# A hybrid decoder layer on one core: the first pair's running sums use one buffer fewer, and the last gate's SiLU stands five products later

## The chip, the cores and the metric

One NeuronCore of a Trainium2 chip runs the whole layer in one launch. The metric is the device time of one execution in microseconds (us). The engines are named as the profile names them: PE is TensorE, DVE is VectorE, ACT is ScalarE, POOL is GpSimd, and SP issues most of the DMAs. Each engine works through its own instructions in a fixed order; an instruction that waits holds up all that stand behind it on its engine.

## The reference

One sequence of 1024 tokens, width 1024, float32. The layer is a SwiGLU half-step, a mixing step, and a second SwiGLU half-step; each has a norm before and after, and shift, scale and gate from a conditioning vector `c`:

```python
c_act = silu(c); mod = c_act @ w_ada + b_ada          # nine rows of 1024
f = (silu(h @ w_gate) * (h @ w_up)) @ w_down          # 1024 -> 2816 -> 1024
x = x + 0.5 * ga1 * rms_norm(f, g_post_ff1)
attn = sliding_window_attention(q, k, v, sinks)       # 8 heads, window 128
ssm = s5_ssm(u, ...)                                  # 32 groups, 64 complex states each
x = x + ga2 * rms_norm(concat(norm(attn), norm(ssm)) @ w_out, g_post_mix)
f = swiglu(h, w2_gate, w2_up, w2_down)
x = x + 0.5 * ga3 * rms_norm(f, g_post_ff2)
```

## The kernel before

**Precision and products.** Every large float32 product is done as three matmuls of a faster format: an operand is split into a high part (an ACT cast, L69) and a low part (a DVE subtraction, L70), and `mm3` (L74 to L76) multiplies high by high, high by low and low by high. The low part of the weights is needed by the third matmul, L76.

**Gate and up projections.** `GateUp` computes them with Strassen's scheme in Winograd's form: the activations stand as 2x2 blocks (512 tokens by 512 channels), the weights too, and a pair of 128-column output tiles (u = 0, 1) needs seven products of 12 matmuls each instead of eight. The first pair is done plainly (`first`); all others go through `rest`, one product after the other in the order "1", "5", "6", "2", "7", "3", "4". Products 1, 6, 7 and 4 add up in one PSUM bank (chain 0), and between them the partial sum is copied out: product 1's by ACT L470 into buffer `c11`, product 5's by L472 into `c22`, product 6's by L474 into `c12`. So the matmuls of product 6 may not begin before L470 has read the bank, and those of product 7 not before L474 has. "Product 6" in the change's words is the sixth in order, product "3".

**Running sums.** The down projection uses the same scheme, so the four result blocks of a pair are stored together with four sums of them. `sums` makes them on DVE (L429, in the order s3, s1, s2, s4) and SP stores them. For the first pair `first_done(1)` calls it, ahead of `rest`, with high priority in the scheduler.

**Buffers.** The blocks and sums live in eight buffers h0 to h7 that `o_rot` hands out in turn. In the first feed-forward the first pair's blocks take h0 (a11), h1 (a12), h2 (a21), h3 (a22), and the four sums h4 to h7; the next request, `c11` of `rest`, gets h0 again. The second feed-forward does the same, one place on: a11 is in h7 there and so is `c11`. A later pair takes exactly eight buffers, so the relation repeats.

**Order.** Inside `rest` each product's steps are pinned in the order written: the conversion of the weights three products ahead (`conv`), the product, a hook. Elsewhere a scheduler that simulates the program chooses each engine's order from dependences and priorities; a change in one place can so move instructions in another. The h buffers also serve the attention's split probabilities in mixing (`at_turn`, L785 and L70), where the state-space steps (`ss_state`, L893 to L916, DVE and POOL) run beside attention; `at_values` multiplies the split probabilities by the values (L74 to L76).

**The last gate.** `hook3` loads `c` once more through POOL (L117), takes its SiLU on ACT (L118, 128x1024), loads the last eight rows of `w_ada` through POOL (L162) and reduces them on DVE (L166) from the tenth product on.

Of the kernel before, what the change touches and what calls it, by code (L numbers as in the profile page):

```python
# [30 lines left out]
def tile_layer(ctx: ExitStack, tc: tile.TileContext, a: dict, out: bass.AP, stage: str = "all"):  # L31
# [12 lines left out]
    def slot(tag, shape, dt=F32):  # L44
        uid[0] += 1
        return sb.tile([P] + list(shape), dt, tag=tag, name=f"{tag}_{uid[0]}")
# [18 lines left out]
    def names(c, *idx):  # L65
        return tuple(f"{c}{i}" for i in idx)
# [31 lines left out]
    o_rot = Rot(*names("h", *range(8)))  # L98
# [15 lines left out]
    def load_c(eng):  # L114

        crow = slot("c0", [D])
        tc.keep_in_program_order(eng.dma_start(crow, a["c"].partition_broadcast(P)))  # L117
        act.activation(crow, crow, AF.Silu)  # L118
        return crow
# [40 lines left out]
    def ada_load(j, tag):  # L160
        w = slot(tag, [D])
        pool.dma_start(w, a["w_ada"][j])  # L162
        return w

    def ada_block(j, w, crow=crow):
        return dve.tensor_tensor_reduce(w, w, crow, 1.0, b_ada[:, j : j + 1], MUL, ADD, modc[:, j : j + 1])  # L166
# [9 lines left out]
    def gate_row(n, v, half):  # L176
        g = ggc[:, n, :]
        if half:
            dve.scalar_tensor_tensor(g, mod(v), 0.5, gains[:, 2 * n + 1, :], op0=MUL, op1=MUL)
        else:  # L180
            dve.tensor_tensor(g, mod(v), gains[:, 2 * n + 1, :], op=MUL)

    def gate_store(n):
        pt = bank(tr_rot(), [P])
        pe.transpose(pt[0:8, :], ggc[:, n, :], ident)
        act.copy(rows[:, n, :], pt[0:8, :])
        pool.dma_start(row_d[n].rearrange("(k p) -> k p", p=P), rows[:, n, :])
# [171 lines left out]
    class GateUp:  # L359
# [49 lines left out]
        def first_done(self, r):  # L409
            for f in range(2):  # L410
                s = slot(o_rot(), [512])
                act.activation(s, self.pb[r, 0, f], AF.Silu)
                dve.tensor_tensor(s, s, self.pb[r, 1, f], op=MUL)
                self.result(0, r, f, s)
            if r == 1:
                with tc.high_priority():
                    self.sums(0, [slot(o_rot(), [512]) for _ in range(4)])


        def result(self, pair, r, f, s):  # L420
# [1102 lines left out]

    def hook3(i):

        if not last_c:
            last_c.append(load_c(pool))
        while last_ada and len(last_raw) < 3:
            j = last_ada.pop(0)
            last_raw.append((j, ada_load(j, rest_rot())))  # L1530
        if last_raw and i > 8 and i % 2:
            ada_block(*last_raw.pop(0), last_c[0])
        if i == 40:
            gate_row(2, 8, True)
        if i == 44:
            gate_store(2)

    g2.rest(lambda i: pinned(hook3, i), pinned)
    down(2, a["w2_d"], None, lambda i: None, lambda: None)

# [72 lines left out]
```

## Time and profile before

| what | us |
|---|---|
| median of 3 runs (1717.0 to 1725.35) | 1717.06 |
| the profiled execution, its own time | 1718.82 |
| its span, first to last instruction | 1717.0 |
| PE busy in the span | 1652.9 (96%) |
| DVE, ACT, POOL busy | 1264.6, 804.3, 124.8 |

The profiled execution's own time is 1.82 us more than its span, and 1.76 us more than the median. The stages in the span: the first feed-forward to about 690 us (its first pair until about 83 us), mixing to about 1060, the second feed-forward from there (its first pair until about 1112). A row of the timeline gives start, duration, engine, line, operation, names and shapes; in brackets the idle time before it on its engine and what ended it. `x4` behind a row stands for four instructions in one row, whose duration then runs from the first start to the last end. Granted clock 1.00 is 2.4 GHz, 0.50 is 1.2 GHz.

### The profile page before, as it was taken

The page shows a single profiled execution, that of the slowest core. Times are in us where ns is not written, and L with a number is a line of the kernel's source. Part 1 is how long each engine was busy: PE and PEld are TensorE (multiplying, and loading weights), DVE is VectorE, ACT ScalarE, POOL GpSimd, SP SyncE. Part 2 cuts the span into 40 slices and gives each one's busy share as a digit, 9 for nine tenths or more (in the row PEclk, how much of TensorE's full clock was granted, in tenths as well). Part 3 has the DMA queues.
Part 4 walks back from the last instruction along what each step waited for, and adds up shares of the span by engine and source line. Part 5 has one row for each costly group of instructions (what it writes and reads, how often), then busy time and mean ns, then how long its engine had stood idle before and what let it go on. Part 6 is the DMA issues. An engine that isn't in the chain of part 4 may idle for free.

```text
span 1717.0 us, 22221 instructions
## 1 busy us (share of the span) xinstructions
PE 1652.9 (96%) x7669; PEld 1355.8 (79%) x7669; DVE 1264.6 (74%) x2470; ACT 804.3 (47%) x1654; POOL 124.8 (7%) x147
## 2 busy tenths in 40 slices
PE   5999999999999999899979998999999999999998
PEld 4878888787788878688757876878888888888886
DVE  7989997788779878735589378768666566678586
ACT  5633333553344557736555257633333333344562
POOL 0011100001100000000015044000000000000001
PEclk9999999999999999999989998999999999999999
DMA  9176752234395734410333126243232223494324
GB/s 377 42 257 239 244 187 93 104 129 149 128 368 183 232 115 147 150 37 13 96 90 87 49 76 197 84 172 117 104 117 92 93 92 120 154 375 125 110 97 161
DMA packets 112065, 249.08 MB, mean 145 GB/s; under 512 B 12088, under 2 KB 27744, under 8 KB 111952
## 3 DMA queue, kind: packets, MB, share of 16 engines
q1 hardware_dynamic: 102224, 214.12, 36.2%
q0 software_dynamic: 9152, 32.49, 5.6%
q8 instruction: 60, 0.98, 0.2%
q10 hardware_dynamic: 576, 1.05, 0.2%
q14 instruction: 53, 0.43, 0.1%
HBM read 187.87 MB, written 59.75 MB: 144 GB/s over the span
## 4 chain that ended last, share of the span: by engine, by line
PE 51%; DVE 4%; DMA 2%; ACT 1%; issue 1%; POOL 1%; SPq 0%; DVEq 0%; ACTq 0%; POOLq 0%
PE b L76 15%; PE b L75 15%; PE b L74 15%; PE b L751 1%; PE b L839 1%; PE b L841 1%; PE b L840 1%; PE b L785 1%; DMA r<-in_w_gu 1%; PE b L930 0%; PE b L205 0%; DMA w<-in_w_out 0%; ACT a L69 0%; POOL a L913 0%; PE b L926 0%
## 5 line engine op out<-in xcount | busy, mean ns | idle before, releaser
L74 PE MATMUL b<-a,w 128*128 128x512 f32 x1260 | 489.3, 393 | 15.1 <-ACT h L470 9.0
L75 PE MATMUL b<-a,w 128*128 128x512 f32 x1260 | 494.6, 392 | 5.6 <-DVE a L70 5.6
L76 PE MATMUL b<-a,w 128*128 128x512 f32 x1260 | 494.5, 392 | 1.4 <-DVE w L70 1.3
L74 PEld LDWEIGHTS b<-a,w 128*128 128x128 f32 x1260 | 238.0, 189 | 68.6 <-ACT h L470 11.5
L75 PEld LDWEIGHTS b<-a,w 128*128 128x128 f32 x1260 | 238.5, 189 | 56.3 <-DVE a L70 7.0
L76 PEld LDWEIGHTS b<-a,w 128*128 128x128 f32 x1260 | 238.6, 189 | 53.6 <-DVE w L70 3.8
L70 DVE TENSOR_TENSOR w<-r,w 128x512 fp32r<-128x512 f32 (+1 forms) x206 | 142.9, 694 | 137.9 <-ACT w L69 137.6
L75 PE MATMUL b<-w,r 128*128 128x512 f32 x528 | 205.5, 389 | 1.1 <-DVE w L70 1.1
L76 PE MATMUL b<-w,r 128*128 128x512 f32 x528 | 205.4, 389 | 0.0
L74 PE MATMUL b<-w,r 128*128 128x512 f32 x528 | 180.7, 389 | 0.0
L69 ACT CAST w<-r 128x512 fp32r<-128x512 f32 (+1 forms) x210 | 130.2, 623 | 94.3 <-DVE r L334 82.4
L69 ACT CAST r<-a 128x512 fp32r<-128x512 f32 x110 | 68.5, 623 | 149.5 <-PE b L76 107.8
L70 DVE TENSOR_TENSOR r<-a,r 128x512 fp32r<-128x512 f32 x110 | 75.7, 688 | 61.7 <-ACT r L69 61.6
L75 PEld LDWEIGHTS b<-w,r 128*128 128x128 f32 x528 | 99.1, 188 | 22.2 <-DVE w L70 1.6
L74 PEld LDWEIGHTS b<-w,r 128*128 128x128 f32 x528 | 99.1, 188 | 20.6
L76 PEld LDWEIGHTS b<-w,r 128*128 128x128 f32 x528 | 99.1, 188 | 20.5
L69 ACT CAST w<-t 128x512 fp32r<-128x512 f32 (+1 forms) x114 | 69.9, 613 | 83.7 <-DVE t L337 30.4
L70 DVE TENSOR_TENSOR w<-t,w 128x512 fp32r<-128x512 f32 (+1 forms) x114 | 79.7, 699 | 31.5 <-ACT w L69 31.3
L466 DVE TENSOR_TENSOR h<-h,b 128x512 f32<-128x512 f32 x120 | 82.2, 685 | 21.3 <-PE b L76 19.2
L454 ACT ACTIVATE h<-h 128x512 f32<-128x512 f32 x60 | 38.0, 633 | 117.8 <-DVE h L466 117.8
L70 DVE TENSOR_TENSOR w<-a,w 128x512 fp32r<-128x512 f32 x110 | 75.3, 685 | 0.2 <-ACT w L69 0.2
L74 PE MATMUL b<-a,a 128*128 128x512 f32 x182 | 72.2, 399 | 0.1
(376 smaller groups left out, 2554.4 us busy)
## 6 DMA issues: line engine op xcount, KB each, us to landing
r<-in_w_gu SPq DMA_DIRECT2D x88, 512.0 KB, 3.9
g_d<-h SPq DMA_DIRECT2D x154, 256.0 KB, 2.1
a<-g_d SPq DMA_DIRECT2D x110, 256.0 KB, 3.4
q<-in_w_ada POOLq DMA_DIRECT2D x48, 512.0 KB, 4.7
a<-in_w_d SPq DMA_DIRECT2D x88, 256.0 KB, 5.4
a<-in_w_ada SPq DMA_DIRECT2D x16, 512.0 KB, 10.2
a<-in_x SPq DMA_DIRECT2D x12, 512.0 KB, 6.8
x_d<-a SPq DMA_DIRECT2D x12, 512.0 KB, 3.7
```

The costliest lines, as they stand in the source:

```text
L69: act.copy(hi, src)
L70: eng.tensor_tensor(lo, src, hi.bitcast(F32), op=SUB)
L74: pe.matmul(psum, wh, xh, start=first, stop=False, skip_group_check=goes_on)
L75: pe.matmul(psum, wh, xl, start=False, stop=False, skip_group_check=goes_on)
L76: pe.matmul(psum, wl, xh, start=False, stop=last, skip_group_check=goes_on)
L454: act.activation(dst, src, AF.Silu)
L466: dve.tensor_tensor(dst, dst, pb, op=ADD)
L751: pe.matmul(pb[kv][:, m % 2, ks], qT[m][rows, t * P : (t + 1) * P], kT[rows, (t + 1 - nk) * P : (t + 1) * P], start=True, stop=True,)
L785: pe.transpose(pt[:, m, :], pr[4 * kv + m][:, b * P : (b + 1) * P], ident)
L839: pe.matmul(pb, hh, wh, start=k == 0, stop=False)
L840: pe.matmul(pb, hh, wl, start=False, stop=False)
L841: pe.matmul(pb, hl, wh, start=False, stop=k == NK - 1)
```

## The change

In the first pair s1 = a21 + a22 is written over a21 itself; only three buffers are taken for the sums, so `c11` of `rest` gets the eighth. `hook3` returns at once for the first five products, so the load of `c`, its SiLU and the first loads of `w_ada` stand behind the sixth.

```diff
             if r == 1:
                 with tc.high_priority():
-                    self.sums(0, [slot(o_rot(), [512]) for _ in range(4)])
+                    self.sums(0, [self.st[1, 0]] + [slot(o_rot(), [512]) for _ in range(3)])
...
     def hook3(i):
 
+        if i < 5:
+            return
         if not last_c:
             last_c.append(load_c(pool))
```

DVE, first feed-forward, the end of the first pair (a name begins with the tile's tag: `h0` is buffer h0; w2 is the weights of product 6, w3 of product 2, w0 of product 7). Before:

```order
L70 TENSOR_TENSOR w2_143_705<-t0_142_703,w2_143_705 128x512
L70 TENSOR_TENSOR a6_160_821<-q2_4_101,a6_160_821 128x512
L70 TENSOR_TENSOR a7_161_824<-q3_5_102,a7_161_824 128x512
L429 TENSOR_TENSOR h6_156_805<-h0_138_688,h2_152_796 128x512
L429 TENSOR_TENSOR h4_154_803<-h2_152_796,h3_153_799 128x512
L429 TENSOR_TENSOR h5_155_804<-h4_154_803,h0_138_688 128x512
L429 TENSOR_TENSOR h7_157_806<-h1_139_692,h5_155_804 128x512
L70 TENSOR_TENSOR w3_168_854<-r1_135_682,w3_168_854 128x512
L339 TENSOR_TENSOR r0_134_680<-r1_135_682,r0_134_680 128x512
L70 TENSOR_TENSOR w0_171_873<-r0_134_680,w0_171_873 128x512
```

The same place of the changed kernel:

```order
L70 TENSOR_TENSOR w2_143_705<-t0_142_703,w2_143_705 128x512
L70 TENSOR_TENSOR a6_159_820<-q2_4_101,a6_159_820 128x512
L70 TENSOR_TENSOR a7_160_823<-q3_5_102,a7_160_823 128x512
L429 TENSOR_TENSOR h5_155_804<-h0_138_688,h2_152_796 128x512
L70 TENSOR_TENSOR w3_167_853<-r1_135_682,w3_167_853 128x512
L339 TENSOR_TENSOR r0_134_680<-r1_135_682,r0_134_680 128x512
L429 TENSOR_TENSOR h2_152_796<-h2_152_796,h3_153_799 128x512
L429 TENSOR_TENSOR h4_154_803<-h2_152_796,h0_138_688 128x512
L429 TENSOR_TENSOR h6_156_805<-h1_139_692,h4_154_803 128x512
L70 TENSOR_TENSOR w0_170_872<-r0_134_680,w0_170_872 128x512
```

The weights' split for product 2 and one sum of weights moved between the first and the second running sum; the second sum writes h2, which it reads. The second feed-forward has the same new order.

DVE in mixing, about 884 to 892 us of the span before: the state-space step of group 0 (L913 to L915), the probabilities of attention tile 7 (L774, scaled) and of tile 6 (L70, split for `at_values`). Before:

```order
L914 TENSOR_TENSOR a5_1280_7685<-a5_1280_7685,q2_1260_7614 128x512
L772 RECIPROCAL s1311_7792<-s1311_7792 128x8
L804 TENSOR_REDUCE t1_1319_7877<-t0_1316_7852 128x128
L915 TENSOR_TENSOR a8_1315_7843<-a4_1279_7684,a5_1280_7685 128x4x127
L774 TENSOR_SCALAR a17_1303_7768<-a17_1303_7768,s1311_7792 128x256 x2
L774 TENSOR_SCALAR c0_1304_7769<-c0_1304_7769,s1311_7792 128x256 x2
L774 TENSOR_SCALAR a17_1303_7768<-a17_1303_7768,s1311_7792 128x256 x2
L774 TENSOR_SCALAR c0_1304_7769<-c0_1304_7769,s1311_7792 128x256 x2
L897 TENSOR_TENSOR a4_1279_7684<-b5_1334_7919,q3_1283_7688 128x512
L70 TENSOR_TENSOR h0_1323_7888<-b0_1321_7882,h7_1322_7887 128x512
```

The same place of the changed kernel:

```order
L914 TENSOR_TENSOR a5_1279_7684<-a5_1279_7684,q2_1259_7613 128x512
L70 TENSOR_TENSOR h7_1322_7887<-b0_1320_7881,h6_1321_7886 128x512
L772 RECIPROCAL s1310_7791<-s1310_7791 128x8
L70 TENSOR_TENSOR h1_1325_7896<-b1_1323_7890,h0_1324_7895 128x512
L915 TENSOR_TENSOR a8_1314_7842<-a4_1278_7683,a5_1279_7684 128x4x127
L897 TENSOR_TENSOR a4_1278_7683<-b5_1333_7918,q3_1282_7687 128x512
L70 TENSOR_TENSOR h3_1328_7905<-b2_1326_7899,h2_1327_7904 128x512
L70 TENSOR_TENSOR h5_1331_7914<-b3_1329_7908,h4_1330_7913 128x512
L774 TENSOR_SCALAR a17_1302_7767<-a17_1302_7767,s1310_7791 128x256 x2
L774 TENSOR_SCALAR c0_1303_7768<-c0_1303_7768,s1310_7791 128x256 x2
L774 TENSOR_SCALAR a17_1302_7767<-a17_1302_7767,s1310_7791 128x256 x2
```

All four splits of tile 6 now stand ahead of the eight scalings of tile 7.

POOL in mixing, the state-space step of group 1 (its result goes to a9; a8 held group 0's, which PE reads, and is cleared by L916 for group 2). Before:

```order
L894 MEMSET a6_1281_7686 128x4
L913 TENSOR_TENSOR a6_1281_7686<-a4_1279_7684,q3_1283_7688 128x512
L914 TENSOR_TENSOR a6_1281_7686<-a5_1280_7685,q3_1283_7688 128x512
L915 TENSOR_TENSOR a9_1335_7946<-a6_1281_7686 128x4x127
L916 MEMSET a8_1393_8187 128x4 x2
```

The same place of the changed kernel:

```order
L894 MEMSET a6_1280_7685 128x4
L916 MEMSET a8_1392_8186 128x4 x2
L913 TENSOR_TENSOR a6_1280_7685<-a4_1278_7683,q3_1282_7687 128x512
L914 TENSOR_TENSOR a6_1280_7685<-a5_1279_7684,q3_1282_7687 128x512
L915 TENSOR_TENSOR a9_1334_7945<-a6_1280_7685 128x4x127
```

The clearing of a8 moved ahead of group 1's three operations.

## Rows read from the trace of the kernel before

**Rows 1.** Busy time by stretch: the stretch and its length, busy us (and instructions) of PE, PEld, DVE, ACT, POOL, then the granted clock, the DMA share and GB/s.

```profile
0.00:100.00 100.00, 78.38 (x376) 66.13 (x377) 82.70 (x207) 53.64 (x115) 4.12 (x13) 0.95 0.59 225
...
300.00:400.00 100.00, 98.73 (x447) 79.98 (x447) 83.20 (x158) 49.88 (x105) 7.46 (x14) 1.00 0.38 132
...
800.00:900.00 100.00, 88.73 (x482) 69.32 (x481) 64.48 (x187) 56.35 (x196) 6.93 (x11) 0.93 0.26 79
...
1100.00:1200.00 100.00, 95.33 (x412) 78.08 (x412) 79.36 (x126) 39.78 (x69) 4.25 (x8) 0.98 0.38 133
1300.00:1400.00 100.00, 100.00 (x443) 82.81 (x442) 64.94 (x99) 34.17 (x60) 0.00 (x0) 1.00 0.34 119
```

**Rows 2.** Who waited for whom, PE over the whole span: us in total, times, longest.

```profile
PE b L74 <- ACT h L470: 9.0, 5, 4.3
...
PE b L75 <- DVE h L70: 5.2, 1, 5.2
```

**Rows 3.** Timeline of PE, first feed-forward: the last matmul of product 5, the first of product 6, the first of product 2.

```profile
88.32 0.39 PE L76 MATMUL b<-a,w 128*128 128x512 f32 x1
91.23 0.50 PE L74 MATMUL b<-a,w 128*128 128x512 f32 x1 [2.52 <-ACT h L470]
...
95.67 0.39 PE L74 MATMUL b<-a,w 128*128 128x512 f32 x1
```

**Rows 4.** Timeline of DVE at the same place: the weights' split for product 6 and the four running sums.

```profile
86.69 0.69 DVE L70 TENSOR_TENSOR w<-t,w 128x512 fp32r<-128x512 f32 x1
...
88.50 2.74 DVE L429 TENSOR_TENSOR h<-h,h 128x512 f32<-128x512 f32 x4
```

**Rows 5.** Timeline of ACT at the same place.

```profile
84.31 1.15 ACT L69 CAST a<-q 128x512 fp32r<-128x512 f32 x2
90.59 0.59 ACT L470 COPY h<-b 128x512 f32<-128x512 f32 x1 [5.13 <-issue]
```

**Rows 6.** Timeline of PE, second feed-forward: the last matmul of product 5 and the first of product 6.

```profile
1117.27 0.39 PE L76 MATMUL b<-a,w 128*128 128x512 f32 x1
1121.91 0.50 PE L74 MATMUL b<-a,w 128*128 128x512 f32 x1 [4.25 <-ACT h L470]
```

**Rows 7.** Busy time by stretch, columns as in rows 1: behind the two stalls (the second row is product 6 of the second feed-forward, whole), and two stretches of mixing.

```profile
92.03:95.67 3.64, 3.64 (x10) 2.83 (x9) 1.69 (x3) 0.78 (x2) 0.00 (x0) 0.53 0.99 361
1121.91:1126.35 4.44, 4.44 (x12) 3.50 (x13) 2.00 (x4) 2.52 (x4) 0.00 (x0) 0.62 0.99 324
880.00:897.00 17.00, 7.61 (x37) 5.72 (x38) 17.00 (x29) 10.00 (x30) 5.93 (x5) 0.62 0.29 91
897.00:912.00 15.00, 15.00 (x104) 11.81 (x103) 14.30 (x18) 8.18 (x19) 6.21 (x7) 0.98 0.45 123
```

**Rows 8.** Timeline of DVE, second feed-forward: the weights' split for product 6 and the four running sums.

```profile
1117.97 0.69 DVE L70 TENSOR_TENSOR w<-t,w 128x512 fp32r<-128x512 f32 x1
...
1119.17 2.74 DVE L429 TENSOR_TENSOR h<-h,h 128x512 f32<-128x512 f32 x4
```

**Rows 9.** Timeline of ACT, second feed-forward; the last row is the cast of weights that now stands right behind the SiLU.

```profile
1121.27 0.59 ACT L470 COPY h<-b 128x512 f32<-128x512 f32 x1 [6.34 <-issue]
1121.75 1.06 ACT L118 ACTIVATE c<-c 128x1024 f32<-128x1024 f32 x1
...
1136.49 0.61 ACT L69 CAST w<-r 128x512 fp32r<-128x512 f32 x1
```

**Rows 10.** Timeline of PE in mixing, the rows that had waited.

```profile
883.00 1.12 PE L888 MATMUL b<-a,q 128*64 128x128 f32 x16 [2.11 <-ACT r L802]
885.91 0.59 PE L806 MATMUL b<-ones,t 128*128 128x1 f32 x2 [1.79 <-DVE t L804]
...
892.36 0.80 PE L75 MATMUL b<-h,a 128*128 128x512 f32 x1 [5.23 <-DVE h L70]
```

**Rows 11.** Timeline of DVE in mixing.

```profile
885.78 0.73 DVE L915 TENSOR_TENSOR a<-a,a 128x508 f32<-128x508 f32 x1
886.43 2.70 DVE L774 TENSOR_SCALAR a<-a,s 128x256 f32<-128x256 f32 x2
...
891.03 0.68 DVE L897 TENSOR_TENSOR a<-b,q 128x512 f32<-128x512 f32 x1
891.63 0.68 DVE L70 TENSOR_TENSOR h<-b,h 128x512 fp32r<-128x512 f32 x1
892.23 0.14 DVE L807 COPY ss_a<-b 128x1 f32<-128x1 f32 x1
...
895.28 0.68 DVE L70 TENSOR_TENSOR h<-b,h 128x512 fp32r<-128x512 f32 x1
```

**Rows 12.** Timeline of POOL in mixing.

```profile
902.53 1.28 POOL L913 TENSOR_TENSOR a<-a,q 128x512 f32<-128x512 f32 x1 [12.69 <-issue]
...
907.11 0.14 POOL L916 MEMSET a<- 128x4 f32 x2
...
919.54 0.14 POOL L916 MEMSET a<- 128x4 f32 x2 [10.66 <-PE b L930]
921.15 6.28 POOL L913 TENSOR_TENSOR a<-a,q 128x512 f32<-128x512 f32 x1 [1.48 <-issue]
```

**Rows 13.** Who waited for whom, PE from 300 to 400 us.

```profile
PE b L74 <- ACT h L470: 1.1, 1, 1.1
```

**Rows 14.** Timeline of POOL ahead of the second feed-forward: the load of `c`.

```profile
1071.69 0.62 POOL L117 DMA_DIRECT2D c<-in_c  x1 [4.79 <-DVE a L255]
```

## The prediction, made before the changed kernel ran

> **What bounds the kernel now.** I read the busy times by stretch first. In the projections PE is the bound: from 1300 to 1400 us it is busy all 100 us, with 443 matmuls at granted clock 1.00, so a matmul costs 100/443 = 0.2257 us and a product of 12 costs 2.71 us. The stretches 0 to 100, 800 to 900 and 1100 to 1200 stand out: lower PE busy time and a granted clock of 0.95, 0.93 and 0.98 [rows 1]. The PE waits name what is behind it: L74 waits for ACT L470, 9.0 us in five waits, longest 4.3, and L75 waits once for DVE L70, 5.2 us [rows 2]. So any gain must come from a place where PE stands still, and from the matmuls that run at the lower clock after it.
>
> The timeline shows two of the L470 waits at the changed place. In the first feed-forward product 6 could have started at 88.55 us (the last matmul of product 5 starts at 88.32 and issues for 0.23), and started at 91.23 [rows 3]. In the second, product 5 ends at about 1117.50 and product 6 starts at 1121.91 [rows 6]. ACT had nothing to do in either case: L470 stood "issue"-idle for 5.13 and 6.34 us [rows 5, 9], and ran when the DVE sums let go of its buffer: `c11` is h0 (h7 in the second feed-forward), which is a11, and the third sum reads a11. The sums run 88.50 to 91.24 and 1119.17 to 1121.91 [rows 4, 8], and L470 starts at 90.59 and 1121.27, when the third of four is done. A second loss follows: behind the wait PE ran at 0.53 (1.2 GHz for nearly all of it) from 92.03 to 95.67, and product 6 of the second feed-forward took 4.44 us for 12 matmuls at 0.62 [rows 7].
>
> **The change part by part.**
>
> *First feed-forward, edit 1.* In the changed kernel `c11` gets the one buffer that the sums no longer take, so L470 waits for product 1 alone. ACT is free at 85.46 [rows 5], product 1 ends at about 86 us (its successor product 5 takes 2.71 and ends at 88.55), so the copy is done by 86.6 and product 6 starts at 88.55. Its weights' split is done at 87.38 [rows 4]. Without the wait the clock stays up, so product 2 starts at 88.55 + 2.71 = 91.26 instead of 95.67 [rows 3]: **4.4 us**. The lower bound is the bare wait, 91.23 - 88.55 = 2.7.
>
> What is late next? In the new order the split for product 2 and one sum of weights (L339) come between the sums. From 88.50 with 0.6 us a step: s3, split, L339, then s1, s2, s4 from 90.30; s2, the third sum, ends at about 91.7. Now `c22` has a11's buffer, so L472 waits for that: 91.7 to 92.3; behind it on ACT are the cast for product 7 to 92.8 and L474 (`c12` in a12's buffer, whose last reader s4 ends at 92.2) to 93.3. Product 7 needs L474 and would start at 91.26 + 2.71 = 93.97. So 0.7 us are to spare; the price if it is gone is what exceeds it.
>
> *Second feed-forward, edit 1.* The split for product 6 runs 1117.97 to 1118.66 [rows 8], later than PE now arrives (1117.50), and the third matmul needs it: a wait of 0.2 to 0.75 us takes the place of the 4.25. The sums follow from 1119.17, the third ends at 1122.34 in the new order, and L472, cast and L474 end at 1123.0, 1123.5 and 1124.0. Product 7 would be ready at about 1123.4 and so waits some 0.6. Before, it began at 1126.35 + 2.71 = 1129.06; now at about 1124.0: **5.0 us**, bounds 4.0 and 5.9 (no such waits). These short waits need not lower the clock: from 300 to 400 PE waited 1.1 us for the same L470 [rows 13] and the granted clock is 1.00 [rows 1].
>
> *Edit 2, the SiLU.* It issues no DMA where the program text suggests: the load of `c` stands at 1071.69 on POOL [rows 14], 40 us ahead of `rest`; POOL's order is not altered there. What moves is ACT L118, 1.06 us from right behind L470 to ahead of the cast at 1136.49 [rows 9]. With L470 gone from 1121 the SiLU would have run in ACT's idle 6.34 us, so it gains nothing of its own. Weights are converted three products ahead of their use, at 2.71 us each, so a cast that stands 1.06 us later is still early and the rest of PE's work covers it. **0**, bounds -0.6 and +1.1 (all of it in the chain L470, L472, L474 against all of it in front of product 9).
>
> *Mixing, a side effect of edit 1.* The rotation of h buffers is shifted and the scheduler orders differently. The dearest place on PE there is 880 to 897: busy 7.61 of 17.00 us at clock 0.62 [rows 7], with waits of 2.11 (ACT L802), 1.79 and 5.23 (DVE L70) [rows 10]. From 897 PE is busy all the time [rows 7], so what it does earlier is won. Before, the first split for tile 6 stood at 891.63 behind L915, all eight L774 (886.43 to 891.03) and L897 [rows 11]. Now it is ahead of them: 891.63 - 4.60 - 0.60 - 0.65 = 885.8, that is 5.8 us earlier, and the fourth at 889.0 against 895.28. On the other side the L774 end some 3.1 us later (at 894.2), and their transposes (L785) wait for them; and DVE is busy 17.00 of 17.00 and then 14.30 of 15.00 [rows 7], so it can't serve all earlier. The price isn't in the trace. From above it is 9.4 us, PE's idle time 17.00 - 7.61; from below -4, if the 3.1 us of the late L774 and one 0.7 us split come fully onto PE. I take **4.5**, nearer to the rows on the wait that goes (5.23) than to either end.
>
> The Trainium skill, "SBUF — State Buffer", section "Who interferes with whom", speaks against this part: VectorE shares one port pair with GpSimd, and one of them locks out the other, so vector work that is moved onto GpSimd's stretch stretches both. The trace agrees as far as it goes: POOL's L913 took 1.28 us at 902.53 and 6.28 at 921.15 for the same shape [rows 12]. By that rule the step of group 1 may cost up to 5.0 us more on POOL, and the sum would be 4.5 + 4.4 with nothing left of mixing, that is near rival B.
>
> *Sum.* 4.4 + 5.0 + 0 + 4.5 = 13.9. The profiled execution's span of 1717.0 becomes 1703.1 and its own time, 1.82 more, 1704.9. That execution is 1.76 above the median of the runs shown, so on the median's scale: 1717.06 - 13.9 = **1703**.
>
> **The rivals.** B: both waits go, mixing gives back as much as it wins. For it: DVE is full there; against it: PE is full from 897 on, so that early work isn't lost. 1717.06 - 9.4 = 1707.7.
>
> C: the waits are handed on. `c22` and `c12` now stand in a11's and a12's buffers, so L472 and L474 are tied to the same sums that held L470, one product later. If PE's turn came 1 to 2 us before the sums were done in both places, and the clock fell with it, the two gains would shrink from 9.4 to some 5: 1712. For it: the second feed-forward is already 0.6 us short by my count; against it: 0.7 us to spare in the first, and 300 to 400 us with 1.1 us of wait and a full clock [rows 1, 13].
>
> D, slower: POOL's L916 clears a8 for group 2 and waits for PE's L930 of group 0 (at 919.54 it had stood 10.66 us for L930 [rows 12]). It is now ahead of group 1's L913 to L915. If PE's L930 comes late because it stands behind matmuls that wait for the late L774, POOL's 1.28 + 1.72 + 1.60 us start late, L913 may take 6.28 instead of 1.28, and PE's matmuls of group 1 wait. It makes the kernel slower when mixing loses more than the 9.4 won; with the 10.66 wait, 5.0 for L913 and 2.3 of matmuls at the lower clock, 18: 1717.06 - 9.4 + 18 = 1725.7. Against it: before, L913 ran only at 902.53, after 12.69 us of idle time [rows 12], and by then L930 of group 0, ahead of it in PE's order, is nearly done.
>
> **How the numbers follow.** Forecast 0.58, own range 1698 to 1707 (mixing 0 to 9, second feed-forward 4.0 to 5.9); B 0.22; C 0.13; D 0.07. A measurement of this kernel can tell 0.5% from no change, 8.6 us: faster is below 1708.5, slower above 1725.6. Faster takes the forecast, and B with some two thirds (it lies 0.8 us inside the line): 0.72. Same takes the rest of B, C, and the half of D that loses less than 18 us: 0.24. Slower: 0.04. The range leaves out most of D, the best cases of the forecast and the far end of C: 1697 to 1711.
>
> **What would show it.** Right: in the changed trace L470 runs at about 86 and 1115 and waits for PE only; the PE waits for L470 lose 6.8 us of 9.0; granted clock 1.00 from 84 to 100 and 1117 to 1127; at most two PE waits under 1 us before product 7, on L474, and a short one on L70 in the second feed-forward. Mixing right: the 5.23 us wait for L70 is gone and PE is busy over 11 us of 880 to 897; wrong: L785 waits for L774 there, or POOL's L916 shows a wait for L930 with L913 behind it. L118 stands near 1131 and nothing waits for the cast behind it. Wrong altogether: a PE wait of over 1.5 us for L474 or L472 behind the sums, or new idle time in a stage that the change doesn't name.

## The result and the profile after

The changed kernel takes 1705.70 us (median of 4 runs, 1704.67 to 1708.09); the kernel before, beside it, 1720.26 (4 runs, 1717.0 to 1725.35). The ratio is 0.9914, with a 95% interval of 0.9893 to 0.9935. In a later set, beside three variants, the two medians are 1708.88 and 1718.11, ratio 0.9946 (0.9929 to 0.9964). So the change makes the kernel faster by 0.5 to 0.9%: 9 to 15 us, with 13.9 forecast. The span of the profiled execution fell from 1717.0 to 1702.9 us.

The busy times by stretch, columns as in [rows 1], with the stretches of [rows 1, 7]:

```profile
84.00:100.00 16.00, 16.00 (x72) 13.28 (x71) 13.88 (x23) 6.49 (x12) 3.90 (x7) 1.00 0.87 305
880.00:897.00 17.00, 14.90 (x77) 11.23 (x76) 17.00 (x29) 9.21 (x19) 5.46 (x5) 0.80 0.25 79
1100.00:1200.00 100.00, 98.09 (x431) 80.19 (x430) 76.51 (x121) 39.63 (x70) 4.23 (x8) 1.00 0.41 145
874.74:891.74 17.00, 11.63 (x53) 8.17 (x50) 17.00 (x31) 10.96 (x32) 6.00 (x5) 0.80 0.37 123
891.74:906.74 15.00, 13.69 (x112) 10.53 (x113) 15.00 (x18) 11.65 (x24) 5.75 (x7) 1.00 0.48 130
```

From 84 to 100 PE is busy all 16 us and the granted clock is 1.00: the stall of [rows 3] and the slow stretch of [rows 7] behind it are gone. At 870 us this trace is 5.26 us ahead of that of before (the lead is explained below), so the stretch 880 to 897 holds later work than that of [rows 7]. The last two rows are shifted by that lead and hold the same work as 880 to 897 and 897 to 912 before. There PE is idle for 5.4 and 1.3 us, where it stood still for 9.4 and 0.0 us before; the granted clock is 0.80 and 1.00, where it was 0.62 and 0.98.

Who waited for whom, PE over the whole span, answering to [rows 2]:

```profile
PE b L74 <- ACT h L69: 2.4, 2, 1.9
PE b L74 <- ACT h L470: 2.3, 3, 1.1
PE b L75 <- DVE h L70: 2.1, 1, 2.1
PE b L930 <- DVE a L915: 1.3, 1, 1.3
PE b L74 <- ACT h L474: 0.7, 1, 0.7
```

The waits for L470 fell from 9.0 us in five to 2.3 in three. The 5.2 us wait for L70 is 2.1, with waits for L69 and L915 that were not there. The wait for L474 is new.

Timeline of ACT, first feed-forward, answering to [rows 5]:

```profile
85.56 0.59 ACT L470 COPY h<-b 128x512 f32<-128x512 f32 x1 [0.57 <-PE b L76]
...
91.30 0.59 ACT L472 COPY h<-b 128x512 f32<-128x512 f32 x1 [4.64 <-PE b L76]
...
92.30 0.59 ACT L474 COPY h<-b 128x512 f32<-128x512 f32 x1
```

L470 waits for PE's product 1 and nothing else. L474, which now needs a12's buffer, ends at 92.89, ahead of product 7.

Second feed-forward, answering to [rows 6, 8, 9]: the rows of PE that had waited, then DVE, then ACT.

```profile
1108.80 0.50 PE L76 MATMUL b<-a,w 128*128 128x512 f32 x1 [0.81 <-DVE w L70]
1114.80 0.50 PE L74 MATMUL b<-a,w 128*128 128x512 f32 x1 [0.68 <-ACT h L474]
```

```profile
1108.05 0.69 DVE L70 TENSOR_TENSOR w<-t,w 128x512 fp32r<-128x512 f32 x1
1108.66 1.29 DVE L70 TENSOR_TENSOR a<-q,a 128x512 fp32r<-128x512 f32 x2
1109.86 0.69 DVE L429 TENSOR_TENSOR h<-h,h 128x512 f32<-128x512 f32 x1
...
1111.67 2.14 DVE L429 TENSOR_TENSOR h<-h,h 128x512 f32<-128x512 f32 x3
```

```profile
1104.85 0.59 ACT L470 COPY h<-b 128x512 f32<-128x512 f32 x1
...
1113.16 0.59 ACT L472 COPY h<-b 128x512 f32<-128x512 f32 x1 [7.20 <-issue]
...
1114.16 0.59 ACT L474 COPY h<-b 128x512 f32<-128x512 f32 x1
...
1123.49 1.04 ACT L118 ACTIVATE c<-c 128x1024 f32<-128x1024 f32 x1
```

Product 6 waits for its weights' split (0.81 us) and product 7 for L474 (0.68), which stands in ACT's order behind L472, and L472 waits for the sums. L118 has moved to 1123.49.

Mixing, answering to [rows 10 to 12]: PE's rows that had waited, DVE, POOL.

```profile
878.78 0.50 PE L74 MATMUL b<-h,a 128*128 128x512 f32 x1 [1.94 <-ACT h L69]
...
882.36 0.80 PE L75 MATMUL b<-h,a 128*128 128x512 f32 x1 [2.10 <-DVE h L70]
```

```profile
881.62 0.68 DVE L70 TENSOR_TENSOR h<-b,h 128x512 fp32r<-128x512 f32 x1
...
884.08 1.27 DVE L70 TENSOR_TENSOR h<-b,h 128x512 fp32r<-128x512 f32 x2
885.28 0.60 DVE L774 TENSOR_SCALAR a<-a,s 128x256 f32<-128x256 f32 x2
```

```profile
897.18 0.14 POOL L916 MEMSET a<- 128x4 f32 x2 [11.52 <-PE b L930]
899.16 1.27 POOL L913 TENSOR_TENSOR a<-a,q 128x512 f32<-128x512 f32 x1 [1.84 <-issue]
```

All four splits run ahead of the L774. L916 does wait 11.52 us for PE, and L913 behind it takes 1.27 us.

**Where along the span the time went.** One instruction looked up in both traces gives the lead there: the same instruction of ACT (a line, and which one of that line) starts so much earlier than in the trace of before. The table gives the change of the lead between such marks: the first feed-forward's stall (from 60.54 to 129.56 us of before, to the third L470), the end of the down projection (598.85 to 630.54, L610 to L156), mixing and what follows it (870.14 to 1110.21, L770 to L412) and the second stall (1110.21 to 1171.53, L412 to L454). Minus is time won, in us. It takes in the kernels of the experiments below, except the two with high priority; "order in mixing" says which of the two orders of DVE in the change's section the kernel has.

| kernel | first stall | 599 to 631 | mixing, to 1110 | second stall | order in mixing |
|---|---|---|---|---|---|
| changed | -4.37 | +0.63 | -4.86 | -4.02 | new |
| changed, again | -4.38 | +3.32 | -0.92 | -4.02 | new |
| sums only | -4.37 | +1.09 | -1.32 | -4.00 | new |
| rotation set back | -4.39 | +2.80 | -0.31 | -4.05 | new |
| first only | -4.37 | +0.63 | -2.98 | +0.99 | new |
| same buffer | +0.73 | +1.06 | -2.18 | +1.11 | new |
| next buffer | +0.72 | +0.92 | -5.13 | +2.02 | nearly the new one |
| second only | +0.03 | +0.57 | +2.10 | -4.77 | old |
| SiLU only | +0.04 | +5.03 | +3.58 | +0.62 | old |
| rotation only | -1.57 | +0.10 | +1.04 | +0.02 | old |
| another order of dealing | -4.38 | +2.83 | +0.59 | -4.14 | old |

Over this one trace of before, the removal of the first stall gives 4.37 to 4.39 in each row of the table that has it. That of the second gives 4.00 to 4.14 where the first is removed as well, and 4.77 in "second only"; that difference was not looked into. The other two columns scatter by up to 5 us between traces; between the two traces of the changed kernel alone by 2.7 and 3.9.

### The profile page after: what moved, and what is told of

Its sections match the earlier page's. It is cut to its first block, busy times and chain, and to the rows that moved or that the text cites. A ratio compares the mean times of both kernels' runs of the same rounds, so it can differ in the third digit from the quotient of the medians.

```text
span 1702.9 us, 22218 instructions
## 1 busy us (share of the span) xinstructions
PE 1649.9 (97%) x7669; PEld 1353.3 (79%) x7669; DVE 1264.4 (74%) x2470; ACT 803.6 (47%) x1654; POOL 120.7 (7%) x147
## 4 chain that ended last, share of the span: by engine, by line
PE 50%; DVE 5%; ACT 2%; DMA 1%; issue 1%; SPq 0%; POOL 0%; DVEq 0%; ACTq 0%; POOLq 0%
PE b L76 15%; PE b L75 15%; PE b L74 15%; PE b L751 1%; PE b L839 1%; PE b L841 1%; DVE a L70 1%; PE b L840 1%; PE b L930 1%; PE b L785 1%; PE b L926 1%; ACT a L69 0%; PE b L205 0%; DMA r<-in_w_gu 0%; DMA w<-in_w_out 0%
## 5 line engine op out<-in xcount | busy, mean ns | idle before, releaser
L70 DVE TENSOR_TENSOR w<-r,w 128x512 fp32r<-128x512 f32 (+1 forms) x206 | 142.9, 694 | 128.6 <-ACT w L69 128.3
L69 ACT CAST w<-r 128x512 fp32r<-128x512 f32 (+1 forms) x210 | 130.2, 623 | 91.8 <-DVE r L334 82.1
L69 ACT CAST r<-a 128x512 fp32r<-128x512 f32 x110 | 68.5, 623 | 148.9 <-PE b L76 112.0
L70 DVE TENSOR_TENSOR r<-a,r 128x512 fp32r<-128x512 f32 x110 | 75.7, 688 | 60.3 <-ACT r L69 59.9
L69 ACT CAST w<-t 128x512 fp32r<-128x512 f32 (+1 forms) x114 | 69.9, 613 | 87.4 <-DVE t L337 33.5
L70 DVE TENSOR_TENSOR w<-t,w 128x512 fp32r<-128x512 f32 (+1 forms) x114 | 79.7, 699 | 32.4 <-ACT w L69 32.1
L454 ACT ACTIVATE h<-h 128x512 f32<-128x512 f32 x60 | 38.0, 633 | 117.8 <-DVE h L466 117.8
L70 DVE TENSOR_TENSOR w<-a,w 128x512 fp32r<-128x512 f32 x110 | 75.4, 685 | 0.4 <-ACT w L69 0.4
```

The source lines that it names most:

```text
L69: act.copy(hi, src)
L70: eng.tensor_tensor(lo, src, hi.bitcast(F32), op=SUB)
L454: act.activation(dst, src, AF.Silu)
```

## The experiments

**The first feed-forward alone, the second alone.** The edit, in the first kernel (the second has `g_ds[1]` and no change of the rotation):

```diff
-self.sums(0, [self.st[1, 0]] + [slot(o_rot(), [512]) for _ in range(3)])
+self.sums(0, ([self.st[1, 0]] if self.g_d is g_ds[0] else [slot(o_rot(), [512])]) + [slot(o_rot(), [512]) for _ in range(3)])
...
-    g1.rest(hook1, pinned)
+    g1.rest(hook1, pinned); o_rot.i += 1
```

> The in-place sum in the first feed-forward alone (the second takes four buffers again; the SiLU edit stays in; the rotation of the h buffers is set back by one before mixing). My theory, three separate terms (first stall 4.4, second stall 4.0, order in mixing about 4): PE's 2.5 us wait for L470 at 88 us is gone, the 4.25 us one at the second feed-forward is back, the 5.2 us wait of L75 for L70 in mixing stays away, and the time is 8.5 us under the kernel before (7 to 10). If the moved order in mixing gave nothing: 4.4 under. If the order in mixing follows the rotation of the buffers, as I wrote: the 5.2 us wait is back and it is 4.4 under as well.

> The in-place sum in the second feed-forward alone (the SiLU edit stays in). My theory: PE's 2.5 us wait for L470 at 88 us and the 5.2 us wait for L70 in mixing are there as before, the 4.25 us wait for L470 is replaced by about 0.8 (L70) and 0.7 (L474), and the time is 4.0 us under the kernel before (3 to 5). If the gain in mixing came with any in-place sum: 8 under.

Measured: the first alone 1711.65 us against 1720.79 (ratio 0.9950, 0.9936 to 0.9963), the second alone 1714.85 (0.9957, 0.9944 to 0.9971). In the first, PE waits again in the second feed-forward and the wait for L70 in mixing stays short (1.8 us); in the second it is the other way round. Timeline of PE, first alone, and PE's waits, second alone:

```profile
1116.45 0.80 PE L74 MATMUL b<-a,w 128*128 128x512 f32 x1 [5.07 <-ACT h L470]
```

```profile
PE b L75 <- DVE h L70: 5.2, 1, 5.2
...
PE b L74 <- ACT h L470: 4.7, 4, 2.5
```

So there are separate terms, and the one in mixing comes with the first feed-forward's edit, although the rotation was set back. The second alone gains 5.9 us by the medians, more than the 4.0 expected; in its trace the stall is worth 4.77 and the rest of the span is no better than before.

**The order in mixing without the removed stalls.**

```diff
-self.sums(0, [self.st[1, 0]] + [slot(o_rot(), [512]) for _ in range(3)])
+self.sums(0, [slot(o_rot(), [512]) for _ in range(4)]); o_rot.i += 1
```

> The kernel before with one buffer of the rotation skipped behind the four sums of each first pair: c11 then takes a12's buffer, whose last reader is the fourth sum. No wait is removed at L470 (each should be 0.6 us longer), but the scheduler puts the four splits of tile 6 ahead of the L774 as in the changed kernel. My theory: the order in mixing alone is worth about 4 us, the longer waits cost 1.2, so about 3 us under the kernel before (1 to 4), with the 5.2 us wait for L70 replaced by about 2. If the order in mixing is worth nothing: 1 us over.

Measured: 1718.90 us against 1720.79, ratio 0.9989 (0.9979 to 0.9999). Timeline of PE, first feed-forward, and PE's wait in mixing:

```profile
92.73 0.50 PE L74 MATMUL b<-a,w 128*128 128x512 f32 x1 [3.22 <-ACT h L470]
```

```profile
PE b L75 <- DVE h L70: 1.8, 1, 1.8
```

The wait for L470 grew from 2.52 to 3.22 us, as a sum of 0.6 us more should do. The wait in mixing is the short one and the lead over mixing grew by 5.13, of which the longer stalls (0.72 and 2.02) took back half. The second stall grew by more than the 0.6 us expected. In this trace the new order wins in mixing without any removed stall, and the median agrees; the next experiment but one has the same order and does not.

**The SiLU edit alone, and the sums alone.** The one kernel has the edit of `hook3` and four buffers for the sums, the other the reverse.

> The SiLU edit alone. My theory: no term in the sum, 0 us (within 1); the 4.25 us wait for L470 stays, L118 moves behind it to a place where PE does not wait. If the SiLU held the chain of copies behind L470: 1 us faster, with product 2 or 7 of the second feed-forward starting earlier. If the load of c moved and disturbed something: slower.

> The in-place sum in both feed-forwards, without the SiLU edit. My theory: all of the gain, as the changed kernel: 13 us under the kernel before (11 to 15), order on PE, DVE and POOL as in the changed kernel, L118 behind a copy of the second feed-forward, in ACT's idle time. If the SiLU edit has a part: L118 (1.06 us) in front of L472 makes product 7's wait for L474 of 0.7 us in the changed kernel longer, up to 1.7, and the gain 1 us smaller.

Measured: the SiLU alone 1720.59 against 1720.79 us, ratio 1.0000 (0.9988 to 1.0012). The sums alone 1710.60 against 1719.64, ratio 0.9952 (0.9933 to 0.9971), 9.0 us, less than the 11 to 15 expected, and second stall -4.00, as in the changed kernel with -4.02. So the SiLU edit has no part in the second feed-forward. That the sums alone came out smaller than the first result of the changed kernel was settled by running that one again (below).

**The free buffer, or the writing in place?**

```diff
-self.sums(0, [self.st[1, 0]] + [slot(o_rot(), [512]) for _ in range(3)])
+self.sums(0, [self.st[1, 0]] + [slot(o_rot(), [512]) for _ in range(3)]); o_rot.i += 1
```

> Everything as in the changed kernel, but one buffer of the rotation is skipped behind the three that the sums take, so that c11 is a11's buffer again. If the free buffer is what removes the stalls (my theory): PE's waits for L470 of 2.5 and 4.3 us are back, with the slow matmuls behind them, so 9 us of the gain are gone; what is left is what this kernel's own order in mixing makes (0 to 5), so 0 to 5 us under the kernel before. If writing s1 in place shortens the sums or frees PE by itself: 9 to 14 us under.

Measured: 1722.39 us against 1719.64, ratio 1.0013 (0.9999 to 1.0027). Timelines of PE and ACT:

```profile
92.19 0.59 PE L74 MATMUL b<-a,w 128*128 128x512 f32 x1 [2.65 <-ACT h L470]
```

```profile
99.19 0.58 ACT L474 COPY h<-b 128x512 f32<-128x512 f32 x1 [4.49 <-DMA g_d<-h]
```

With a11's buffer under `c11` again, the stalls are back (+0.73 and +1.11 in the table), and nothing is left of the gain. Writing s1 in place wins nothing; the buffer that it frees does. The expectation was missed in one part: this kernel has the new order in mixing, which was to leave 0 to 5 us of gain, and the median is 2.75 us over that of before. The second row shows one more edge of the edit: the buffer that `c12` gets here is a21's, which holds s1, and L474 waits 4.49 us for its store.

**Buffer numbers, or the scheduler's timing?** The kernel before with `o_rot.i += 7` behind `g1.rest(hook1, pinned)`, and the changed kernel with `o_rot.i += 1` there.

> The kernel before with seven buffers of the rotation skipped between the first feed-forward's last pair and mixing, so that mixing gets the buffer numbers of the changed kernel, and nothing else. If the numbers make the new order in mixing, as my prediction has it: the 5.2 us wait of L75 for L70 goes to about 2 and the time is 4 us under the kernel before. If the order comes from the scheduler's own timing of the first feed-forward, whichever buffers are dealt (my theory now): the 5.2 us wait stays and the time is the same within 1 us.

> The changed kernel with one buffer of the rotation skipped between the first feed-forward and mixing, so that mixing gets the buffer numbers of the kernel before. If the numbers made the new order: the 5.2 us wait of L75 for L70 is back and the time is 8 to 9 us under the kernel before. If the scheduler's timing made it (my theory, after the run with the rotation alone): the wait stays at about 2 us, and the time is that of the changed kernel within 2 us.

Measured: the rotation alone 1718.62 against 1719.64 us, ratio 0.9993 (0.9981 to 1.0004); the rotation set back 1710.52 against 1718.11, ratio 0.9948 (0.9931 to 0.9964). Timelines of PE, first the one, then the other:

```profile
889.34 0.79 PE L75 MATMUL b<-h,a 128*128 128x512 f32 x1 [5.24 <-DVE h L70]
```

```profile
884.22 0.79 PE L75 MATMUL b<-h,a 128*128 128x512 f32 x1 [0.69 <-DVE h L70]
...
887.74 0.80 PE L75 MATMUL b<-h,a 128*128 128x512 f32 x1 [1.02 <-DVE h L70]
```

The long wait is there with the new numbers and the old first feed-forward, and away with the old numbers and the new one. So the numbers with which mixing begins do not make the order.

**The changed kernel again.**

> The changed kernel once more, beside the kernel before and the two variants below. My theory: the two stalls are worth 8.4 us in every execution (lead of 4.4 at 90 us and 4.0 more at the second feed-forward), and what mixing adds differs between executions of the same order, with the time that PE stays at half clock behind 885 us: so 8 to 15 us under the kernel before in the median, over 8.6 in most executions. If the SiLU edit has a part of its own, which the run of the sums alone (8 us under) leaves open: nearer 14 under in all of them.

Measured: 1708.88 us (1705.53 to 1713.94) against 1718.11, ratio 0.9946 (0.9929 to 0.9964), and a trace of 1712.2 us, 9.3 longer than the first of the same program. The table has the difference: 2.7 us at 599 to 631 and 3.9 in mixing, none at the stalls; 1.9 more lie between 631 and 870, and 0.8 ahead of 60 us and between the stalls' marks. Busy time by stretch in mixing, columns as in [rows 1], the first trace of the changed kernel and the second. The second is 5.3 us behind at 870 (leads of 5.26 and -0.06), so its stretches lie 5.32 us later and hold the same work:

```profile
869.68:879.68 10.00, 6.80 (x52) 5.12 (x47) 10.00 (x24) 9.29 (x32) 0.23 (x1) 1.00 0.47 157
879.68:891.68 12.00, 9.83 (x40) 7.17 (x41) 12.00 (x24) 5.98 (x16) 5.78 (x5) 0.72 0.28 87
891.68:906.68 15.00, 13.69 (x110) 10.53 (x112) 15.00 (x18) 11.65 (x24) 5.75 (x7) 1.00 0.48 130
```

```profile
875.00:885.00 10.00, 6.94 (x52) 5.13 (x48) 10.00 (x24) 9.29 (x32) 0.23 (x1) 0.97 0.46 157
885.00:897.00 12.00, 10.22 (x26) 7.12 (x27) 12.00 (x24) 5.08 (x14) 5.73 (x5) 0.50 0.28 89
897.00:912.00 15.00, 15.00 (x98) 11.85 (x98) 12.87 (x16) 8.89 (x19) 5.33 (x7) 0.85 0.30 76
```

Over the three stretches PE is idle for 6.7 us in the first trace (3.20 + 2.17 + 1.31) and 4.8 in the second (3.06 + 1.78 + 0). Yet by the granted clocks the first stood at 1.2 GHz for about 6.7 us (0.28 of 12 us, doubled), the second for about 17 (0.03 of 10, 0.50 of 12 and 0.15 of 15, doubled): both estimates from these rows. The six executions of this set go the same way: the slowest two, 1713.94 and 1713.72 us, have a mean granted clock of 0.984, the fastest, 1705.53, has 0.988.

**Two tries to win more.** Another order of dealing buffers behind the sums:

```diff
+...; i = o_rot.i; o_rot.turn = {i + 1: i + 4, i + 2: i + 1, i + 3: i + 2, i + 4: i + 3}
```

`o_rot` looks a place up in `turn` before it hands out the buffer.

> The changed kernel with the next four buffers dealt in another order behind the sums: c22 takes a22's buffer (last read by the second sum), c12 a11's (third sum), instead of a11's and a12's. My theory: L472 and L474 run 0.6 us earlier behind the sums, product 7 of the second feed-forward no longer waits 0.7 us for L474, and the stage gains 4.6 us over the kernel before instead of 4.0; the whole time is within 1 us of the changed kernel but for mixing. If the store of a22 is late, L472 waits for it and PE for L470 or L474: 1 to 3 us over the changed kernel.

Measured: 1712.29 us against 1718.11, ratio 0.9961 (0.9946 to 0.9977). PE's wait for L474 fell from 0.68 to 0.31 us, and the second stall's term is -4.14 instead of -4.02: the small gain went the way expected, by less. It did not show in the time, which is 3.4 us over that of the changed kernel in the same set. This kernel has the old order of DVE in mixing, all eight L774 ahead of the splits, and a PE wait of 5.2 us is back there. So another dealing of the buffers behind the sums, with both stalls still removed, is enough to bring the old order back.

High priority for the transposes and splits of attention, on all tiles and on the last two:

```diff
+            hp = tc.high_priority if n >= 8 else contextlib.nullcontext
...
-                at_turn(n - 2)
+                with hp():
+                    at_turn(n - 2)
```

This is the one for the last two tiles; for all tiles the condition is `n >= 0`.

> The changed kernel with the scheduler's high priority on the transposes and splits of the attention probabilities (at_turn), so that the four casts (L69) of tile 6 stand ahead of the eight exponentials (L770) of tile 7, and its splits earlier on DVE. In the changed kernel PE still waits 1.9 + 0.5 us for those casts and 2.1 us for the splits, partly at half clock. If those waits are the rest of the loss there: 3 to 5 us under the changed kernel, 16 to 19 under the kernel before. If tile 7's later exponentials and scalings take their place: within 1 us of the changed kernel.

> The changed kernel with high priority on the transposes and splits of attention tiles 6 and 7 alone: the casts of tile 6 stand between the exponentials of tile 7, and no other tile's order changes by design. With priority on all tiles the kernel was 23 us slower than the changed one, most of it lost from 790 to 870 us. If that loss came from the earlier tiles: PE's wait of 1.9 us for L69 goes below 1 us and the time is 0 to 4 us under the changed kernel. If any priority on the turns starves the scores on DVE: 3 us or more over it.

Measured: on all tiles 1728.28 us against 1719.64, ratio 1.0046 (1.0029 to 1.0062); on the last two 1716.10 against 1718.11, ratio 0.9982 (0.9974 to 0.9991). Both are slower than the changed kernel, against my theory. PE's waits from 760 to 900 us with priority on all tiles, and the stretch of mixing with priority on two:

```profile
PE b L751 <- ACT w L846: 3.5, 2, 1.8
PE b L785 <- DVE a L774: 3.5, 3, 2.4
```

```profile
885.00:897.00 12.00, 9.99 (x30) 7.15 (x31) 11.59 (x21) 4.36 (x12) 2.51 (x4) 0.50 0.28 89
897.00:905.00 8.00, 8.00 (x28) 6.23 (x28) 3.10 (x4) 0.48 (x1) 0.00 (x0) 0.50 0.03 7
905.00:915.00 10.00, 10.00 (x54) 8.37 (x54) 7.55 (x9) 4.90 (x11) 5.77 (x7) 0.68 0.63 159
```

On all tiles, the transposes (L785) wait for the scalings, and L751 for ACT; that they hold up other work of PE is argued and not shown. On two tiles the single wait for L69 did shrink, to 1.0 us, but PE stayed at half clock for 20 us, of which it was idle for 2. So in this kernel's stretch the clock cost more than the waits.

## Why the prediction was right, and where not

**The sum.** 1703 was forecast, with 1697 to 1711; 1705.7 and, in the second set, 1708.9 were measured. By the second set's difference, 9.2 us, the kernel stands nearer to rival B (9.4 us, both stalls gone and nothing from mixing) than to the forecast; by the first set's, 14.6, it stands at the forecast. The two terms of the stalls make 8.4 us against the trace of before, and what decides between the two cases scatters from one execution to the next. That the first set came within 0.7 us of the forecast is in part luck: the second stall's term came out 1.0 us short, mixing's term had a wrong cause, and 1.0 us was won between 631 and 870 us (leads of 4.26 and 5.26), where nothing was forecast. The base moved too: the median of before, 1717.06 in three runs, is 1720.26 with the fourth, and from there the forecast would read 1706.4. One sum of the prediction is off: where it weighs 5.0 us more on POOL, it writes 4.5 + 4.4 for the two stalls, which it had put at 4.4 and 5.0.

**First feed-forward: right to a tenth.** 4.4 us forecast, 4.37 measured against the trace that the forecast was made from. The chain of copies that was checked for the next delay came out as counted or better: L474 was to end at 93.3 and ended at 92.89, with the whole trace 0.5 us early, and product 7 did not wait.

**Second feed-forward: right in its mechanism, mis-sized by 1 us.** 5.0 us forecast, bounds 4.0 to 5.9, and 4.02 measured. Both new waits were named, and their sizes as rows are a little over mine: 0.81 us where I had 0.2 to 0.75, and 0.68 where I had 0.6. The mis-sized step is the start of the running sums, "the sums follow from 1119.17". In the new order two splits of activations (1108.66, x2) stand between the weights' split and the first sum; before there was one. So the first sum starts at 1109.86, which is 1119.98 in the time of before (the lead is 10.12 there), 0.8 us late. The chain behind it, L472, cast, L474, ends at 1114.75 or 1124.87 instead of 1124.0, and product 7 waits for its end; the wait for L70 ahead of it is covered by that. A short wait also costs PE a little more than its row says, since the row counts from the end of the matmul before (0.39 us behind its start), and the next would have started 0.23 behind it: the matmul of 1108.80 follows an issue at 1107.60, 1.20 us where 0.23 is the normal step, 0.97 us lost and not 0.81. Likewise from 1113.73 to 1114.80: 1.07, or 0.84 lost. The clock stayed at 1.00, as forecast.

**The SiLU: right.** 0 us, and 0.2 by the medians of the edit alone. L118 moved to a place where PE does not wait for it, at 1123.49 and not, as I wrote, near 1131.

**Mixing: the place was right, the cause was wrong, the size stays open.** The step "the rotation of h buffers is shifted and the scheduler orders differently" failed: with the rotation alone the order and the 5.24 us wait are those of before, and with the rotation set back the new order stays. What remains is the other half of that sentence: what the scheduler does in the first feed-forward alters the choices it makes 800 us later. It is not tied to the removed stall: the next buffer and the same buffer have the new order with the stalls, another order of dealing has the old one without them. That is argued from these kernels; the scheduler's own state was not looked at, and which edit gives which order stays open. Of the working, the first split was to come 5.8 us earlier and came 4.75 earlier (881.62, with a lead of 5.26 at 870); the L774 were to end 3.1 us later and ended 1.6 later, since the eight took 2.2 us in place of 4.7, of which the first two alone had taken 2.70 [rows 11]. New waits for L69 (2.4 us) and L915 (1.3) weren't in the sum. On the whole, the six traces with the new order have won 0.3 to 4.9 us over mixing, 2.1 on average, and "next buffer" 5.1. The four traces with the old order beside that of before have lost 0.6 to 3.6; with before's own the five lost 1.5 on average. That makes 3.6 us between the orders, with 4.5 forecast.

The medians say less. What a kernel gained beyond its own two stall columns can be estimated from them:

| set | kernels with the new order | kernels with the old order |
|---|---|---|
| first result | changed 6.2 | |
| with "first only" | first only 5.8, next buffer 4.6 | second only 1.2, SiLU only 0.9 |
| with "sums only" | sums only 0.7, same buffer -0.9 | rotation only -0.5 |
| with "changed, again" | changed 0.8, rotation set back -0.8 | another order of dealing -2.7 |

Within a set the new order is ahead of the old by about 4, 0.4 and 2.7 us; the middle one is lost in the intervals of the ratios. The kernels of one set agree with each other better than two sets of one kernel do. What differs between the sets was not looked into; the last three ran on three different chips. So how much of the 4.5 us the new order is worth stays open between 0 and 4.

**The rivals.** C did not come: the waits that were handed on took 1.5 us in all and left the clock alone. D did not come either: L916 waited for L930 as it was drawn (11.52 us), yet L913 behind it took 1.27 us, the same as the 1.28 of [rows 12], and no matmul of group 1 waited for POOL; PE's 1.3 us wait was for DVE's L915. The rule of the Trainium skill that was weighed there ("SBUF — State Buffer", "Who interferes with whom") fits what the L774 show, in the other direction. Before, the first two took 2.70 us [rows 11] beside these two of POOL:

```profile
885.93 1.71 POOL L914 TENSOR_TENSOR a<-a,q 128x512 f32<-128x512 f32 x1
887.72 1.26 POOL L915 TENSOR_TENSOR a<-a 128x508 f32<-128x508 f32 x1
```

In the changed kernel POOL's L915 is over at 884.69, and the first two, from 885.28, took 0.60. That the port pair is the cause is argued from the overlap alone.

## What to carry to other kernels

When a copy out of PSUM stalls PE though its engine is idle, look at the buffer that it writes: who reads that buffer last decides, and dealing it another buffer is worth the whole stall, and the slow matmuls behind it where the clock had fallen. Check at once which copies inherit the tied buffer and how much later they are needed. Where a scheduler orders the program, an edit in one stage can reorder another: separate the two with a kernel that has the order without the edit, and compare the traces mark by mark, since the total hides terms of both signs. Where one trace is ahead of the other, shift the stretches by the lead, or they hold different work.

## What was not expected of the hardware

Executions of one program differ by up to 13 us within one set (sums only, 1706.83 to 1719.94). In the two traces of the changed kernel, 9.3 us apart, most of it lies in two places. At about 600 us DVE's reductions (L171) wait for rows of `w_ada`, and the splits behind them make PE wait; in the trace of the SiLU edit alone this cost 5.0 us more than in that of before. DVE's and PE's rows there, and the stretch around them in that trace and in the one of before:

```profile
600.92 0.75 DVE L171 CUSTOM_DVE_ANT_0 h<-h,c,cols 128x512 f32<-128x512 f32 x1 [1.22 <-DMA h<-in_w_ada]
602.94 0.50 PE L75 MATMUL b<-w,r 128*128 128x512 f32 x1 [1.04 <-DVE w L70]
605.97 0.79 PE L75 MATMUL b<-w,r 128*128 128x512 f32 x1 [2.06 <-DVE w L70]
```

```profile
595.00:610.00 15.00, 11.90 (x44) 9.04 (x43) 8.15 (x17) 5.39 (x10) 0.00 (x0) 0.84 0.87 269
595.00:610.00 15.00, 13.87 (x62) 11.16 (x61) 8.68 (x18) 7.67 (x14) 0.00 (x0) 1.00 0.73 238
```

PE was idle for 2.0 us more than in the trace of before, and by the granted clock, 0.84 and not 1.00, it stood at 1.2 GHz for about 4.8 of these 15 us (an estimate, 0.16 of 15, doubled), which costs half of that.

The second place is mixing, and there it is the clock: with the same order of instructions and less idle time, PE ran at 1.2 GHz for some 17 us in one execution and 7 in another, as worked out above.

The same holds for the first stall. In the kernel with the rotation alone, PE waits 2.50 us for L470 as before (2.52), but the stretch behind it, which ran at 0.57 from 92 to 96 us in the trace of before, runs at full clock:

```profile
92.00:96.00 4.00, 4.00 (x20) 3.28 (x19) 2.29 (x4) 1.95 (x4) 0.00 (x0) 1.00 0.95 356
```

That is the -1.57 in the table: the wait is paid each time, the slow matmuls behind it are not. So removing this stall is worth 2.8 to 4.4 us, by the execution that one compares with, and one trace does not give the size of a loss of clock.
